# The up stages of a feed-forward block make their own sums of transposed activations

## The chip, the cores and the metric

The program runs on one core of one Trainium2 chip. The metric is the device time of one execution in microseconds (us). TensorE (PE) multiplies, VectorE (DVE) and ScalarE (ACT) prepare its operands and take its results out of PSUM, GpSimd (POOL) does small work and issues some transfers, SyncE (SP) issues most of them. The queues of transfers issued by SP and ACT and the one of POOL are separate, and each engine works through its own instructions in a fixed order.

## What is computed

One layer on 2048 tokens of 1024 values: attention and a recurrent branch (not touched here), then a merge, and a feed-forward block. The part that matters, cut from the reference:

```python
merged = gate_a * (y_a @ proj_a[l]) + gate_b * (y_b @ proj_b[l])
x = x + rms_norm(merged @ w_out[l], post_mix_g[l])

hf = rms_norm(x, pre_ffn_g[l])
u = jnp.square(jax.nn.relu(hf @ w_up[l])) @ w_down[l]
x = x + rms_norm(u, post_ffn_g[l])
```

`hf` is 2048 x 1024, `w_up` 1024 x 4096, all in float32.

## The kernel before

The tokens stand in four groups of 512. For each group the kernel runs its recurrent stage, its attention and its merge (`phase_merge`, which multiplies by `proj_a` and `w_out`). Behind the last group's merge come four stages on halves of two groups: up stage of half 0, down stage of half 0, up stage of half 1, down stage of half 1. The residual steps (`residual_steps`) of a group write the transposed `hf` to DRAM, into `ht[g]`, 128 partitions x 8 blocks x 512 tokens. Those of groups 0 and 1 run beside earlier merges, those of 2 and 3 beside the first down stage.

Float32 operands are split in two parts, `h` and `l` (names that end in `h` and `l`), and each product is three matmuls per block (`mm3`). A split is a cast by ACT and a subtraction by DVE (`split`, or `split_here` where the raw block was loaded into the low part's tile).

An up stage (`phase_up`) multiplies two pairs of column blocks of `w_up` by the two groups of a half with seven products in place of eight. Each takes 12 matmuls, from four blocks of K of 128 rows. On the right-hand side stand two raw halves of the first group (`b1`, tiles `bh` and `bl`), the second group's raw second half (`b22`), and four sums: t1 = g1lo - g0lo, t3 = g1hi - g1lo, t2 = g1hi - t1, t4 = g0hi - t2, where lo and hi are the first and last four blocks of `ht`. The first two products of a step need `bh` and `bl` alone. So the stage begins with eight early pairs of these (the loop over `early`, eight tiles `z`): the first product of a pair is copied to `z` by ACT, the second is added by DVE (`r<-z,ps_u`), and both take turns in two PSUM banks (pool `pd`). Meanwhile the operands of the other five products are made (`operands`), a step or two after each pair. Then comes the main loop with five products per step.

The four sums were made ahead: `combinations` loads four raw blocks of 128 x 512, makes the sums with four subtractions on DVE and stores them in DRAM (`td`) through POOL. That of half 0 runs beside the last group's merge (`early`, with tiles `cmb` in a pool `p1` of its own), that of half 1 beside the first down stage (`beside`). The up stage then loads each sum in two pieces into the low part's tile and splits it there.

`first_half` loads `bl` in four pieces and splits them into `bh` and `bl`. For half 0 it is written behind the merge, ahead of the up stage; for half 1 beside the first down stage. Pools are stacked in on-chip memory, and a tile waits for whatever used its place before. The instructions' order on each engine is set by a scheduler when the program is built, so it is not the order of the code. The last merge's results, four tiles `o0` to `o3` in pool `p0`, are stored to DRAM (`od`) by ACT's queue when the merge is done.

## Time and profile before

| | us |
|---|---|
| median of three runs | 3340.6 (3339.0 to 3341.2) |
| the profiled execution | 3337.6 |
| its span, first to last instruction | 3335.9 |
| last merge, end | about 2034 |
| early pairs of the first up stage | 2034 to 2079 |
| first down stage, end | about 2699 |
| early pairs of the second up stage | about 2699 to 2746 |

The times inside the span are read from the timeline of the profiled execution. Busy time on an engine that is not the bound costs nothing by itself. The waits in front of PE's instructions are what a change can add or take away here. In rows, `L83` is the line in `mm3`, whatever stage calls it, so stages are told apart by tile names: `ps_o` is the merge's product with `w_out`, `ps_u` the up stages', `ps_dn` the down stages'. A row of the waits has the total, the number of times and the longest. In a timeline the bracket at the end of a row gives the engine's idle time before it and what ended it.

### The profile page before, as it was taken

To read this page: it belongs to the slowest core of one execution; us is meant where nothing else is said; L and a number is where in the kernel's file an instruction comes from. 1 tells how busy PE (TensorE), PEld (TensorE's weight loads), DVE (VectorE), ACT (ScalarE), POOL (GpSimd) and SP (SyncE) were. 2 spreads that over 40 slices of the span, in tenths; PEclk is the share of its full clock that TensorE was granted. 3 is DMA by queue.
4 is the path that set the end of the run, shared out by engine and by line. 5 is a ranking of instruction groups with operands and counts; after the bars stand their busy time and mean duration, and the time that the engine had idled before them with its cause. 6 is when DMAs were issued, how large, how long until landed. Compare 5 with 4: busy or idle time off the path is not lost. (4 is left out here: it accounts for less than half of the span.)

```text
span 3335.9 us, 49381 instructions
## 1 busy us (share of the span) xinstructions
PE 3244.5 (97%) x19089; PEld 2608.4 (78%) x19089; DVE 2284.0 (68%) x3814; ACT 1463.2 (44%) x2331; POOL 382.7 (11%) x732
## 2 busy tenths in 40 slices
PE   7999999999999999999999999999999999999998
PEld 6777787777777777777777777888888878888887
DVE  6774656765665774565774675877877787776788
ACT  4434634444644444644434644333431254454432
POOL 2210002111012210012210000111200011100000
PEclk9999999999999999999999999999999999999999
DMA  5224343125263224354224256434756364554444
GB/s 157 80 89 147 98 145 120 61 90 182 91 236 129 69 86 168 106 205 151 83 83 152 87 206 237 131 120 142 268 177 202 106 242 162 169 171 153 141 162 133
DMA packets 166099, 478.43 MB, mean 143 GB/s; under 512 B 17564, under 2 KB 34144, under 8 KB 163176
## 3 DMA queue, kind: packets, MB, share of 16 engines
q1 hardware_dynamic: 110004, 361.97, 32.9%
q0 software_dynamic: 18688, 63.98, 5.0%
q10 hardware_dynamic: 37172, 49.32, 4.1%
q8 instruction: 151, 2.47, 0.3%
q14 instruction: 84, 0.69, 0.1%
HBM read 355.64 MB, written 122.71 MB: 143 GB/s over the span
## 5 line engine op out<-in xcount | busy, mean ns | idle before, releaser
L83 PE MATMUL psd<-hh,whi 128*128 128x512 f32 x1344 | 542.5, 404 | 2.3 <-DVE QA L835 2.3
L83 PE MATMUL psd<-hl,whi 128*128 128x512 f32 x1344 | 539.3, 401 | 0.0
L83 PE MATMUL psd<-hh,wlo 128*128 128x512 f32 x1344 | 536.5, 399 | 0.0
L74 ACT CAST whi<-wraw 128x1024 fp32r<-128x1024 f32 x232 | 243.7, 1050 | 532.7 <-PE psd L83 421.9
L83 PE MATMUL ps_dn<-fop 128*128 128x512 f32 x1920 | 439.7, 390 | 2.1 <-DVE u L1291 1.5
L75 DVE TENSOR_TENSOR wlo<-wraw,whi 128x1024 fp32r<-128x1024 f32 x232 | 283.1, 1220 | 208.9 <-ACT whi L74 188.1
L83 PEld LDWEIGHTS ps_dn<-fop 128*128 128x128 f32 x1920 | 359.4, 188 | 78.6 <-DVE u L1291 2.3
L83 PEld LDWEIGHTS psd<-hh,whi 128*128 128x128 f32 x1344 | 256.1, 191 | 57.5 <-issue 3.4
L83 PEld LDWEIGHTS psd<-hh,wlo 128*128 128x128 f32 x1344 | 255.8, 190 | 54.1 <-issue 3.5
L83 PEld LDWEIGHTS psd<-hl,whi 128*128 128x128 f32 x1344 | 255.8, 190 | 50.8 <-issue 2.1
L83 PE MATMUL ps_dn<-fop,fop 128*128 128x512 f32 x1008 | 228.6, 389 | 0.0
L83 PEld LDWEIGHTS ps_dn<-fop,fop 128*128 128x128 f32 x1008 | 189.3, 188 | 39.2
L1291 DVE TENSOR_TENSOR u<-u,ps_dn 128x512 f32<-128x512 f32 x240 | 160.6, 683 | 54.3 <-PE ps_dn L83 53.8
L895 DVE CUSTOM_DVE_ANT_0 sc<-bias,ps_s 128x640 f32<-128x640 f32 (+4 forms) x128 | 94.1, 735 | 54.6 <-PE ps_s L889 50.6
L74 ACT CAST fop<-wdraw 128x1024 fp32r<-128x1024 f32 x40 | 41.9, 1047 | 191.8 <-DVE u L1291 88.7
L900 ACT ACTIVATE sc<-sc,mn 128x640 f32<-128x640 f32 (+4 forms) x128 | 97.8, 764 | 35.2 <-DVE mn L895 30.1
L74 ACT CAST s12h<-s 128x1024 fp32r<-128x1024 f32 x32 | 33.7, 1054 | 169.5 <-PE ps_u L83 169.5
L1019 PE MATMUL ps_o<-whi,mh 128*128 128x512 f32 x256 | 101.9, 398 | 1.9 <-ACT o L1025 1.9
L83 PE MATMUL ps_p<-yh,whi 128*128 128x512 f32 x256 | 102.1, 399 | 0.7 <-DVE th L985 0.7
L1019 PE MATMUL ps_o<-wlo,mh 128*128 128x512 f32 x256 | 101.8, 397 | 0.7 <-DVE wlo L75 0.7
L83 PE MATMUL ps_p<-yh,wlo 128*128 128x512 f32 x256 | 102.1, 399 | 0.0
L83 PE MATMUL ps_p<-yl,whi 128*128 128x512 f32 x256 | 101.5, 396 | 0.0
(378 smaller groups left out, 6741.8 us busy)
## 6 DMA issues: line engine op xcount, KB each, us to landing
wraw<-in_w_in_dram SPq DMA_DIRECT2D x168, 512.0 KB, 3.7
wraw<-in_w_up_dram SPq DMA_DIRECT2D x80, 512.0 KB, 4.5
ar<-sd SPq DMA_DIRECT2D x21, 1024.0 KB, 4.8
wdraw<-in_w_down_dram SPq DMA_DIRECT2D x40, 512.0 KB, 4.0
araw<-ad SPq DMA_DIRECT2D x40, 512.0 KB, 4.0
gd<-gate ACTq DMA_DIRECT2D x64, 256.0 KB, 2.3
wraw<-in_w_out_dram SPq DMA_DIRECT2D x32, 512.0 KB, 3.7
ad<-r POOLq DMA_DIRECT2D x64, 256.0 KB, 2.4
```

The source lines that it names most:

```text
L74: self.nc.scalar.copy(hi, src)
L75: self.nc.vector.tensor_tensor(lo, src, hi.bitcast(F32), ALU.subtract)
L83: mm = nc.tensor.matmul(ps, l, r, start=start and n == 0, stop=stop and n == last).ins
L895: nc.vector.tensor_tensor_reduce(sc[:, 0:n], bias[:, s0:640], pss[:, c0 : c0 + n], 1.0, 3.0e38, ALU.add, ALU.min, mn,)
L900: nc.scalar.activation(sc[:, 0:n], sc[:, 0:n], AF.Exp, scale=-1.0, bias=mn, accum_out=sm)
L1019: nc.tensor.matmul(ps[t], l[:, k, ts], r[:, k % 2], start=k == 0 and j == 0, stop=k == KB - 1 and j == 2)
L1291: nc.vector.tensor_tensor(u[t][:, ns], u[t][:, ns], ps, ALU.add)
```

## The change

`combinations` and the DRAM tiles `td` are gone, and with them the pool `p1`. Each up stage loads raw blocks: four pieces of 128 x 1024 for the first two blocks of K, issued by SP, and four for the other two, issued by POOL. They go into a second tile of the shape of `z`, `slots`, which existed before in the second up stage only (for sums of its outputs). DVE makes the four sums in place with subtractions of 128 x 1024, with t2 in the last two rows of `z`, and each is split from there. The number of subtracted elements is the same; 4 MB less is stored and 5 MB less loaded in each half.

```diff
--- before.py
+++ after.py
@@ -296,7 +296,6 @@
 
         self.ht = [dp.tile([P, KB, G], F32, name=f"ht{g}") for g in range(self.NG)]
         self.ad = [dp.tile([P, 2, G], F32, name=f"ad{f}") for f in range(FF // P)]
-        self.td = [dp.tile([P, 4, KB // 2, G], F32, name=f"td{h}") for h in range(self.NG // 2)]
         self.sd = [dp.tile([P, len(PARTS), XB, G], F32, name=f"sd{b}") for b in range(BATCHES)]
         self.gd = [dp.tile([P, 2, G], F32, name=f"gd{i}") for i in range(KB)]
         self.yd = [dp.tile([P, G], F32, name=f"yd{p}") for p in range(NP)]
@@ -984,7 +983,7 @@
             self.mm3(ps, [(wh[:, k, c], wl[:, k, c], y[0][:, k], y[1][:, k]) for k in range(NP)])
             nc.vector.scalar_tensor_tensor(t[:, j], t[:, j], 1.0, ps, op0=ALU.add, op1=ALU.mult)
 
-    def phase_merge(self, g, o, between, early=iter(())):
+    def phase_merge(self, g, o, between):
 
         tc, nc, a = self.tc, self.nc, self.a
         with ExitStack() as ctx:
@@ -1001,7 +1000,6 @@
                 self.branches(self.ya, t)
                 nc.vector.tensor_tensor(t, t, self.md[i], ALU.add)
                 self.split(mh[:, 2 * i : 2 * i + 2], ml[:, 2 * i : 2 * i + 2], t)
-                advance(early, 1)
             self.yctx.close()
             self.late = e(tc.tile_pool(name="late", bufs=2, side="right", reuse_waits="tile"))
             for n in range(2):
@@ -1092,22 +1090,6 @@
                     advance(nrm[t], 1)
             yield
 
-    def combinations(self, half, mp, bufs=1):
-
-
-        nc = self.nc
-        KH = KB // 2
-        g0, g1 = (self.ht[2 * half + i] for i in range(2))
-        for k in range(KH):
-            b = mp.tile([P, 4, G], F32, tag="cmb", bufs=bufs, name="cmb")
-            for i, src in enumerate((g0[:, k], g1[:, k], g0[:, KH + k], g1[:, KH + k])):
-                nc.sync.dma_start(b[:, i], src)
-            for o, x, y in ((0, 1, 0), (1, 3, 1), (3, 3, 0), (2, 2, 3)):
-                nc.vector.tensor_tensor(b[:, o], b[:, x], b[:, y], ALU.subtract)
-            nc.gpsimd.dma_start(self.td[half][:, :, k], b)
-            yield
-
-
     def split_here(self, hi, lo):
 
         self.nc.scalar.copy(hi, lo.bitcast(F32))
@@ -1138,20 +1120,23 @@
             bh, bl = self.b1
             B11, B21 = (bh[:, lo4], bl[:, lo4]), (bh[:, hi4], bl[:, hi4])
             z = zp.tile([P, early, G], F32, tag="z", name="z")
+            slots = zp.tile([P, early, G], F32, tag="z", name="slots")
             T = {
                 n: [tb.tile([P, KH, G], F32R, name=n + x) for x in "hl"] for n in ("t4", "b22", "t2", "t3", "t1")
             }
 
             def operands():
-                td, g1 = self.td[half], self.ht[2 * half + 1]
-                for n, src in (
-                    ("t2", td[:, 3]), ("t3", td[:, 1]), ("t1", td[:, 0]), ("b22", g1[:, hi4]), ("t4", td[:, 2])
-                ):
-                    h, l = T[n]
-                    for k in (0, 2):
-                        ks = slice(k, k + 2)
-                        nc.sync.dma_start(l[:, ks].bitcast(F32), src[:, ks])
-                        self.split_here(h[:, ks], l[:, ks])
+                g0, g1 = self.ht[2 * half], self.ht[2 * half + 1]
+                t1, t3, b22, t4 = (slots[:, n : n + 2] for n in range(0, early, 2))
+                t2 = z[:, early - 2 : early]
+                for k in (0, 2):
+                    ks = slice(k, k + 2)
+                    for t, src in ((t1, g0[:, lo4]), (t3, g1[:, lo4]), (b22, g1[:, hi4]), (t4, g0[:, hi4])):
+                        (nc.gpsimd if k else nc.sync).dma_start(t, src[:, ks])
+                    for o, x, y in ((t1, t3, t1), (t2, b22, t1), (t3, b22, t3), (t4, t4, t2)):
+                        nc.vector.tensor_tensor(o, x, y, ALU.subtract)
+                    for n, src in (("t2", t2), ("t3", t3), ("b22", b22), ("t4", t4), ("t1", t1)):
+                        self.split(*(x[:, ks] for x in T[n]), src)
                         yield
 
             def product(l, r, pool, tag):
@@ -1178,7 +1163,6 @@
                 return sums and FIRST <= i < FIRST + BATCHES * XB
 
             if sums:
-                slots = zp.tile([P, early, G], F32, tag="z", name="slots")
                 R = {q: slots[:, n] for n, q in enumerate(("a11", "a12", "a21", "a22", "s1", "s2", "s4"))}
 
             def hidden(src, x, fb, th, out=None):
@@ -1532,13 +1516,10 @@
                 self.phase_rwkv(g)
                 self.phase_attention(g)
                 with ExitStack() as c:
-                    early = iter(())
-                    if g == self.NG - 1:
-                        early = self.combinations(0, c.enter_context(tc.tile_pool(name="p1", bufs=1, reuse_waits="tile")), 2)
                     sp = c.enter_context(tc.tile_pool(name="p0", bufs=2, reuse_waits="tile"))
                     pt = c.enter_context(tc.tile_pool(name="p0p", bufs=2, space=PSUM, reuse_waits="tile"))
                     o = [sp.tile([P, D], F32, tag="o", bufs=GT, name=f"o{t}") for t in range(GT)]
-                    self.phase_merge(g, o, self.after(g, sp, pt), early)
+                    self.phase_merge(g, o, self.after(g, sp, pt))
                     for t in range(GT):
                         self.nc.scalar.dma_start(self.od[g][t], o[t])
             mixing.close()
@@ -1552,7 +1533,6 @@
             def beside(op, pt):
                 for g in (2, 3):
                     yield from self.residuals(g, op, pt)
-                yield from self.combinations(1, op)
                 yield from self.first_half(2, bp)
 
             advance(self.first_half(0, bp))
```

Three places in the order of instructions matter for the prediction. In the rows, a name before the arrow is written and the ones behind it are read; wait names are semaphores: DMAHW of transfers issued by SP and ACT, DMASW of those issued by POOL.

SP at the end of the last merge, before, with the waits (`wraw<-in_w_out` are the merge's weights, `bl<-ht` the first group's raw blocks, `t2l<-td` and `t3l<-td` the stored sums):

```order
L62 DMA wraw<-in_w_out_dram 128x1024 [waits DMAHW2_49,DMAHW0_49,DVE_49]
L1164 DMA wraw<-in_w_up_dram 128x1024 [waits DMAHW3_49,DVE_49]
L1164 DMA wraw<-in_w_up_dram 128x1024 [waits DMAHW4_49,DVE_49]
L62 DMA wraw<-in_w_out_dram 128x1024 [waits DMAHW6_49,DVE_49]
L1121 DMA bl<-ht_335 128x1024 [waits DMASW2_49]
L1121 DMA bl<-ht_335 128x1024 [waits DMAHW5_49]
L1121 DMA bl<-ht_335 128x1024
L62 DMA wraw<-in_w_out_dram 128x1024 [waits DMAHW7_49,DMAHW0_49,DVE_49]
L1121 DMA bl<-ht_335 128x1024
L1164 DMA wraw<-in_w_up_dram 128x1024 [waits DMAHW1_49]
L62 DMA wraw<-in_w_out_dram 128x1024 [waits DMAHW3_49,DMAHW2_49,DVE_49]
L1153 DMA t2l<-td_371 128x1024 [waits DMAHW7_49,PE_49]
```

The same place in the changed program:

```order
L62 DMA wraw<-in_w_out_dram 128x1024 [waits DMAHW5_49,DVE_49]
L62 DMA wraw<-in_w_out_dram 128x1024 [waits DMAHW1_49,DVE_49]
L62 DMA wraw<-in_w_out_dram 128x1024 [waits DMAHW4_49,DVE_49]
L1103 DMA bl<-ht_335 128x1024 [waits DMAHW3_49,DMAHW7_49,DMAHW2_49,Activation_49]
L1103 DMA bl<-ht_335 128x1024
L1103 DMA bl<-ht_335 128x1024 [waits DMAHW5_49]
L1103 DMA bl<-ht_335 128x1024 [waits DMAHW6_49]
L1135 DMA slots<-ht_335 128x1024 [waits DVE_49,PE_49]
L1135 DMA slots<-ht_336 128x1024 [waits DMAHW0_49]
L1135 DMA slots<-ht_336 128x1024 [waits DMAHW1_49]
L1135 DMA slots<-ht_335 128x1024
L1149 DMA wraw<-in_w_up_dram 128x1024 [waits DMAHW3_49,DVE_49]
```

The loads of `bl` stood between the last weights of the merge, and the first waited for a transfer of POOL, the store of `cmb`. Now they stand behind all of them, and the first waits for three transfers of SP or ACT and for ACT. By the semaphores' counts in the built program two of those are the stores `od` of `o0` and `o3`, and the instruction of ACT is the last copy into `o3`. In on-chip memory `bl` lies at 64.7 to 80.7 KB of each partition in both programs; `cmb` lay at 72.7 to 88.7 KB and `o0` to `o3` at 88.7 to 104.7 KB, and now `o0` to `o3` lie at 72.7 to 88.7 KB.

ACT at the end of the last merge, before (`o` are the merge's results, `whi` casts of its weights, `bh` the cast of `bl`, the first four `o` copies are those of the first half of columns):

```order
L74 CAST s12h<-wraw 128x1024
L74 CAST s3h<-wraw 128x1024
L74 CAST whi<-wraw 128x1024 x2
L1113 CAST bh<-bl 128x1024
L1025 COPY o_18791<-ps_o 128x512
L1113 CAST bh<-bl 128x1024
L1025 COPY o_18792<-ps_o 128x512
L1025 COPY o_18793<-ps_o 128x512
L1025 COPY o_18794<-ps_o 128x512
L74 CAST whi<-wraw 128x1024
L1113 CAST bh<-bl 128x1024 x2
L74 CAST whi<-wraw 128x1024 x2
```

and in the changed program, from the last of those four copies to the first up product's copy `z`:

```order
L1023 COPY o_18789<-ps_o 128x512
L74 CAST whi<-wraw 128x1024 x3
L1023 COPY o_18786<-ps_o 128x512
L1524 DMA od_0_331<-o_18786 128x1024
L1023 COPY o_18787<-ps_o 128x512
L1023 COPY o_18788<-ps_o 128x512
L1023 COPY o_18789<-ps_o 128x512
L1524 DMA od_1_332<-o_18787 128x1024
L1524 DMA od_2_333<-o_18788 128x1024
L1524 DMA od_3_334<-o_18789 128x1024
L1095 CAST bh<-bl 128x1024 x4
L1197 COPY z<-ps_u 128x512
```

The casts of `bh` stood ahead of and among the merge's first `o` copies. Now they stand behind all `o` copies and their stores.

DVE in the early part of the first up stage, before (`r<-z,ps_u` ends a pair, `a1l` and `s12l` are weights of coming pairs, `t2l`, `t3l` and `t1l` the low parts of operands):

```order
L1189 TENSOR_TENSOR r<-z,ps_u 128x512
L75 TENSOR_TENSOR a1l<-wraw,a1h 128x1024
L1192 TENSOR_TENSOR r<-r 128x512
L1114 TENSOR_TENSOR t2l<-t2l,t2h 128x1024
L1189 TENSOR_TENSOR r<-z,ps_u 128x512
L75 TENSOR_TENSOR s12l<-wraw,s12h 128x1024
L1192 TENSOR_TENSOR r<-r 128x512
L1114 TENSOR_TENSOR t2l<-t2l,t2h 128x1024
L1114 TENSOR_TENSOR t3l<-t3l,t3h 128x1024
L1189 TENSOR_TENSOR r<-z,ps_u 128x512
L1114 TENSOR_TENSOR t3l<-t3l,t3h 128x1024
L1114 TENSOR_TENSOR t1l<-t1l,t1h 128x1024
```

in the changed program, from the same instruction on:

```order
L1173 TENSOR_TENSOR r<-z,ps_u 128x512
L75 TENSOR_TENSOR a1l<-wraw,a1h 128x1024
L1176 TENSOR_TENSOR r<-r 128x512
L1137 TENSOR_TENSOR slots<-slots 128x1024
L1137 TENSOR_TENSOR z<-slots 128x1024
L1137 TENSOR_TENSOR slots<-slots 128x1024
L1137 TENSOR_TENSOR slots<-slots,z 128x1024
L75 TENSOR_TENSOR t2l<-z,t2h 128x1024
L1173 TENSOR_TENSOR r<-z,ps_u 128x512
L75 TENSOR_TENSOR t3l<-slots,t3h 128x1024
L75 TENSOR_TENSOR b22l<-slots,b22h 128x1024
L1176 TENSOR_TENSOR r<-r 128x512
```

and further on, from the end of the fourth pair to that of the fifth:

```order
L1173 TENSOR_TENSOR r<-z,ps_u 128x512
L75 TENSOR_TENSOR b22l<-slots,b22h 128x1024
L1176 TENSOR_TENSOR r<-r 128x512
L75 TENSOR_TENSOR a1l<-wraw,a1h 128x1024
L1137 TENSOR_TENSOR slots<-slots 128x1024
L1209 TENSOR_TENSOR s_19615<-wraw 128x512
L1137 TENSOR_TENSOR z<-slots 128x1024
L1137 TENSOR_TENSOR slots<-slots 128x1024
L1137 TENSOR_TENSOR slots<-slots,z 128x1024
L75 TENSOR_TENSOR t2l<-z,t2h 128x1024
L1173 TENSOR_TENSOR r<-z,ps_u 128x512
```

Four subtractions and the split of t2 stand between the end of the first pair and that of the second. Four more, with a split and weights, stand between the fourth and the fifth.

## Prediction

> **What bounds the kernel now.** I read the page first, then the busy time by stage, then who TensorE waits for there.
>
> ```profile
> span 3335.9 us, 49381 instructions
> PE 3244.5 (97%) x19089; PEld 2608.4 (78%) x19089; DVE 2284.0 (68%) x3814; ACT 1463.2 (44%) x2331; POOL 382.7 (11%) x732
> ```
>
> TensorE (PE) is busy for 97% of the span and its matmuls are the same before and after, so an edit can only change how long PE waits. The table of stages (length; busy time and count of PE, PEld, DVE, ACT, POOL; granted clock; DMA share; GB/s) shows where such time is to be had in the stages that the change touches: last merge (two rows), early part of the first up stage, the stretch of the first down stage that holds combinations, early part of the second up stage.
>
> ```profile
> 1950.00:1990.00 40.00, 39.68 (x183) 31.61 (x180) 30.85 (x39) 10.88 (x11) 2.17 (x3) 1.00 0.79 282
> 1990.00:2034.20 44.20, 42.03 (x181) 33.48 (x181) 20.76 (x20) 17.31 (x21) 0.71 (x1) 1.00 0.63 235
> 2034.20:2078.90 44.70, 43.74 (x193) 35.87 (x192) 31.33 (x37) 26.60 (x36) 3.80 (x7) 1.00 0.77 284
> 2500.00:2570.00 70.00, 69.59 (x311) 57.28 (x311) 55.80 (x79) 15.08 (x17) 2.92 (x4) 1.00 0.62 211
> 2701.00:2745.80 44.80, 42.21 (x184) 33.98 (x182) 35.62 (x41) 30.39 (x43) 3.54 (x5) 1.00 0.83 309
> ...
> PE ps_o L1019 <- ACT o L1025: 1.9, 2, 1.4
> PE ps_p L83 <- DVE th L985: 0.3, 1, 0.3
> PE ps_o L1019 <- DVE wlo L75: 0.3, 1, 0.3
> ...
> PE ps_dn L83 <- DVE u L1291: 0.4, 1, 0.4
> ```
>
> The stages that lose work have almost no PE idle time to give: 0.3 + 2.2 us in the merge, 0.4 us in the down stage. The waits in the last four rows (three of the merge, one of the down stage: total, times, longest) add up to 2.9 us. The early parts, which receive work, are as full of PE work, and DVE there is busy 31.3 of 44.7 us and 35.6 of 44.8 us.
>
> **What is removed.** 32 subtractions, 32 loads, 8 stores and the 16 loads of stored sums. They lie beside PE work, so their removal is worth at most those 2.9 us. The largest piece, 1.9 us, is ACT's copies of the merge's result, which PE waits for because they are queued behind a cast of `bh`:
>
> ```profile
> 2011.37 1.04 ACT L1113 CAST bh<-bl 128x1024 fp32r<-128x1024 f32 x1 [5.55 <-DMA bl<-ht]
> 2012.32 0.58 ACT L1025 COPY o<-ps_o 128x512 f32<-128x512 f32 x1
> ```
>
> ACT's new order has these copies first, so this goes. The other waits are for DVE work with combinations between its pieces; they go too. Gain: 2.9 us, between 0 and 4 (pipeline refill after each wait included).
>
> **What moves without being named in the change: the loads of `bl`.** `bl` holds the first group's raw blocks for the first up stage. Its place in the partition is 64.7 to 80.7 KB in both programs. Before, the combination buffers `cmb` lay there; now the merge's results `o0` and `o3` (72.7 to 80.7 KB) do, since the pool `p1` below them is gone. The order shows what follows: the first `bl` load waits for two stores on hardware queues (`od` of `o0` and `o3`, by their semaphore values) and for ACT. Before, these loads went out 30 us ahead of need:
>
> ```profile
> 2004.72 1.53 SPq L1121 DMA_DIRECT2D bl<-ht  x3
> 2007.48 0.44 SPq L1121 DMA_DIRECT2D bl<-ht  x1
> ...
> 2033.40 1.64 ACT L1025 COPY o<-ps_o 128x512 f32<-128x512 f32 x3 [0.40 <-PE ps_o L1019]
> 2034.46 2.08 ACTq L1543 DMA_DIRECT2D od<-o  x3
> ...
> L83 PE MATMUL ps_u<-bh,a1h x8: 389/389/389, 2034.3 to 2039.0; 128*128 128x512 f32 x8
> ...
> wraw<-in_w_out_dram SPq DMA_DIRECT2D x32, 512.0 KB, 3.7
> od<-o ACTq DMA_DIRECT2D x16, 512.0 KB, 3.5
> x<-xr POOLq DMA_DIRECT2D x16, 512.0 KB, 4.4
> td<-cmb POOLq DMA_DIRECT2D x8, 1024.0 KB, 5.7
> bl<-ht SPq DMA_DIRECT2D x8, 512.0 KB, 9.8
> ```
>
> PE starts the first up product at 2034.3, straight after the merge's last matmul; the last `o` copy ends at 2035.0, and the last three `od` stores are issued one after the other from 2034.5 on, the last about 2035.5. In the new program, on the same clock: that store lands 3.5 us later (median row), with 0.5 us for the ones ahead of it, 2039.5. The first `bl` load lands 3.7 us after that (the row of a load of this size), 2043.2. ACT casts it (1.04 us), DVE subtracts (1.23 us, the row of 2012.45 below), so the product's second matmul, the first that needs the low part, can go at 2045.4; with the one matmul that went ahead of it (0.2 us) the product starts 10.9 us late. The other three pieces follow about 1.25 us apart (512 KB at the 421 GB/s of the row below), faster than PE uses them. **Wait added: 10.9 us.** Below: the store and the load each at 2.6 us, the fastest landing of an `od` store, give 8. Above: the time from issue to cast of the old `bl` loads, 6.65 us (2004.72 to 2011.37), gives 14. Nothing covers it: PE's next work in order is this product, and every up and down stage stands behind it.
>
> ```profile
> 2012.45 1.23 DVE L1114 TENSOR_TENSOR bl<-bl,bh 128x1024 fp32r<-128x1024 f32 x1 [5.37 <-ACT bh L1113]
> ...
> 2045.40:2050.80 5.40, 5.40 (x25) 4.47 (x24) 1.00 1.03 421
> ...
> L1114 DVE TENSOR_TENSOR bl<-bl,bh x4: 1217/1222/1226, 2012.4 to 2018.6; 128x1024 fp32r<-128x1024 f32 x4
> ...
> L1543 ACTq DMA_DIRECT2D od<-o x4: 326/392/783, 504.7 to 507.0; - x4
> ...
> DMA to landing us min/median/max: 2.6/2.6/2.6
> ```
>
> The Trainium skill ("DMA: Bandwidth & Descriptors", where it derives the bandwidth figures) holds that a core's memory side binds at about 358 GB/s. By it each piece would take 1.46 us, an estimate, and the sum would grow by about 1 us; the row's 421 GB/s speaks against it and decides.
>
> A wait of this length also costs clock. After a wait of 2.84 us elsewhere (its row, then the stretches behind it) the granted clock was half for 6.8 us:
>
> ```profile
> 621.73 1.92 PE L596 MATMUL ps_t<-X,NA 32*32 32x32 f32 x64 [2.84 <-DVE X L575]
> ...
> 621.50:628.30 6.80, 6.58 (x75) 0.50 0.15 58
> 628.30:635.10 6.80, 6.80 (x118) 1.00 0.28 80
> ```
>
> Half of 6.8 us is 3.4; some of it falls while PE waits for the second piece anyway, so I take **2 us**, between 0 and 3.4. The Trainium skill ("TensorE: Matmul & The Clock Gate", on the HAM clock gate) gives one busy window of about 3.4 us at half clock, which by itself would be 1.7 us (an estimate); the row is longer.
>
> **What is added on DVE.** In each up stage eight subtractions of 128x1024 enter the early part, where PE runs eight pairs of products of 5.49 us. One costs 1.22 us, 1.14 when another follows (the starts in DVE's timeline below); 9.1 us in all, against DVE idle time of 13.4 and 9.2 us in the stage rows, of which one pair's length is its wait for the first pair. The average nearly fits; the order doesn't. DVE's `r<-z,ps_u` frees the second of two banks, and PE needs it 2.74 us into the next pair but one product later.
>
> ```profile
> 2050.85 0.69 DVE L1189 TENSOR_TENSOR r<-z,ps_u 128x512 f32<-128x512 f32 x1 [0.21 <-PE ps_u L83]
> 2051.45 1.22 DVE L1114 TENSOR_TENSOR t3l<-t3l,t3h 128x1024 fp32r<-128x1024 f32 x1
> 2052.59 1.22 DVE L1114 TENSOR_TENSOR t1l<-t1l,t1h 128x1024 fp32r<-128x1024 f32 x1
> ...
> 2072.54 0.69 DVE L1189 TENSOR_TENSOR r<-z,ps_u 128x512 f32<-128x512 f32 x1 [0.89 <-PE ps_u L83]
> ...
> 2078.03 0.69 DVE L1189 TENSOR_TENSOR r<-z,ps_u 128x512 f32<-128x512 f32 x1 [3.42 <-PE ps_u L83]
> ...
> 2716.50 0.69 DVE L1189 TENSOR_TENSOR r<-z,ps_u 128x512 f32<-128x512 f32 x1 [2.11 <-PE ps_u L83]
> ...
> 2721.93 0.69 DVE L1189 TENSOR_TENSOR r<-z,ps_u 128x512 f32<-128x512 f32 x1 [3.42 <-PE ps_u L83]
> ```
>
> First up stage, counted from the end of pair 0: `r`, `a1l`, the square, four subtractions, `t2l` and the next `r` take 0.6+1.14+0.6+4.56+1.14+0.69 = 8.7 us; PE wants the bank at 5.49+2.74 = 8.2: 0.5 us of wait. The second four stand between `r` of pair 3 (done at 18.1) and `r` of pair 4: six operations of 128x1024 and two blocks of 0.6 ahead of `t2l` and `r`, 9.9 us, so 28.0 against 0.5+22.0+2.74 = 25.2: 2.8 us. Together **3.3 us**. Second up stage, from `r` of pair 2 at 2716.5: 0.6, eight operations of 1.14 and `r` end at 2726.9; pair 3 ends at 2721.9 and the bank is wanted at 2724.6. ACT's copy of `z` behind the new casts holds the first product too; pair 4 ends 2.7 us late, of which 1.3 us replaces an old wait. The second four then hold `r` of pair 5 to 2740.7 against 2737.9. Together **4.2 us**. The lower bound of both is 0, if the loads are early and the order slacker than counted. The upper: the second set of raw blocks is loaded through POOL, the last only after `t1l` has been read out. I counted 4.4 us to landing, the row of POOL's 512 KB transfers; at 9.8 us, the worst load row, 4 us more each, 7.3 and 8.2.
>
> **Sum.** -2.9 + 10.9 + 2 + 3.3 + 4.2 = +17.5 us. The profiled execution took 3337.6 us in all (span 3335.9), so 3355.1 there; the median of the three runs is 3.0 us above that execution, so I say 3358. With all ends low (gain 4): 8 - 4 = +4; with all high: 14+3.4+7.3+8.2 = +33.
>
> **Rivals.** Forecast: wait, clock and both backlogs, 3358, chance 0.5. *Wait without backlog*: DVE's idle time (13.4 and 9.2 us) covers the 9.1 us; for it stand the averages, against it the counted order: 3340.6 - 2.9 + 10.9 + 2 = 3351, chance 0.24. *POOL's loads late*: the second four subtractions stand in DVE's queue for `t1`, and everything behind them: 3358 + 8 = 3366, chance 0.17. *Relief only* (not slower): the loads of `bl` still come early. It decides at one point, which transfers the two semaphore values of the held load stand for: if they were older ones than `od` of `o0` and `o3`, the loads would go out behind the last `w_out` load (2017.5 in the row below) and land 10 us ahead of need. Then 3340.6 - 2.9 = 3337.7, with DVE covered; counting the semaphores' updates in the built program speaks against it, chance 0.05. *Small wait*: 8 us, no clock loss, no backlog, 3346; chance 0.04.
>
> ```profile
> 2017.54 0.33 SPq L62 DMA_DIRECT2D wraw<-in_w_out_dram  x1
> ```
>
> **Range and chances.** A difference of 0.2%, 6.7 us, is about what a measurement of this kernel tells from no change, so slower begins at 3347.3. Forecast and late loads lie wholly above, the wait alone for nine parts in ten: 0.87 slower, 0.11 within, 0.02 faster. The ends of the sum are 3345 and 3374; the range, 3346 to 3369, leaves out relief, the far end of late loads and what needs several low or high ends at once.
>
> **What would show it.** The first `bl` load issued after 2036 on the old clock instead of 2004.7, and a PE wait of 8 to 14 us ahead of the first `ps_u<-bh` product, with a granted clock of 0.5 behind it; no 1.9 us wait of `ps_o` for ACT; in each early part one or two PE waits of 1 to 3 us ended by `r<-z,ps_u`; merge and down stages otherwise unchanged. If the first up product follows the merge at once, the main term is wrong; if PE's early parts show no wait for `r`, the backlog is.

## The result and the profile after

The changed kernel takes 3368.0 us (median of four runs, 3366.3 to 3369.6) against 3340.4 us before: 27.6 us more, ratio 1.0084 with a 95% interval of 1.0068 to 1.0100. It is slower, inside the range, and 10 us slower than forecast.

The page of the changed kernel: PE has the same 19089 matmuls and is busy for 8.1 us longer than before (3244.5 us there). The rest of the added time went into waits.

```profile
span 3367.9 us, 49344 instructions
PE 3252.6 (97%) x19089; PEld 2613.7 (78%) x19089; DVE 2284.4 (68%) x3798; ACT 1465.5 (44%) x2331; POOL 380.4 (11%) x732
```

To see where, both traces are cut at the same matmuls (length; busy time and count of PE, PEld, DVE, ACT, POOL; granted clock; DMA share; GB/s). The rows are the last merge (first to last product `ps_o`), the first early part (to the first product with `t2h`), the first down stage with what follows it up to the second up stage, and the second early part (first product of that stage to the first with `t2h`). Before:

```profile
1987.33:2034.03 46.70, 44.53 (x192) 35.54 (x191) 23.43 (x23) 18.20 (x22) 0.71 (x1) 1.00 0.64 238
2034.03:2078.90 44.87, 43.91 (x194) 36.04 (x192) 31.33 (x37) 26.77 (x36) 3.80 (x7) 1.00 0.77 285
...
2340.18:2693.44 353.26, 351.07 (x1577) 290.19 (x1576) 281.94 (x367) 98.52 (x132) 34.05 (x66) 1.00 0.56 186
2693.44:2745.85 52.41, 49.77 (x218) 40.15 (x216) 43.04 (x53) 35.07 (x57) 7.24 (x12) 1.00 0.84 309
```

And in the changed kernel:

```profile
1988.37:2031.69 43.32, 43.32 (x192) 35.85 (x191) 15.19 (x13) 14.94 (x18) 0.00 (x0) 1.00 0.44 152
2031.69:2097.77 66.08, 48.36 (x195) 38.09 (x193) 45.14 (x49) 31.24 (x40) 6.01 (x11) 0.90 0.58 204
...
2359.02:2710.16 351.14, 350.45 (x1578) 290.37 (x1577) 273.91 (x351) 98.41 (x132) 30.27 (x62) 1.00 0.50 164
2710.16:2773.84 63.68, 53.21 (x218) 41.71 (x216) 52.54 (x61) 36.21 (x57) 9.45 (x16) 0.95 0.69 236
```

The profiled spans differ by 32.0 us (3367.9 - 3335.9). Merge -3.4, first early part +21.2, down stage -2.1, second early part +11.3 give 27.0. Another 3.9 us lie behind the last matmul (the section on the closing drain has its cause). The remaining 1.1 us are spread over stretches without a changed instruction, 1.0 of it ahead of this merge. (The two profiled executions stand 1.7 above their median and 2.8 us below theirs, hence 32.0 here and 27.6 between the medians.)

The rows also divide what each early part grew by. In the first, PE's busy time is 4.4 us longer and its idle time 16.8 us; in the second, 3.4 and 7.8 us. The matmuls are the same and the granted clock is below 1 in both (0.90 and 0.95), so the longer busy time is an estimate of what the lower clock cost there (the ends of matmuls are modelled).

What ended PE's waits in the changed kernel (total, times, longest):

```profile
PE ps_u L83 <- ACT z L1197: 13.9, 5, 4.9
PE ps_u L83 <- ACT bh L1095: 10.4, 1, 10.4
...
PE ps_u L83 <- DVE r L1173: 1.6, 2, 1.0
...
PE ps_u L83 <- DVE bl L1096: 0.5, 1, 0.5
```

The wait for `bh` is one wait in one place; the waits for the copies `z` are five, in both early parts. The merge's waits for ACT's `o` are gone. The timeline around the wait for `bh`:

```profile
2037.47 1.75 SPq L1103 DMA_DIRECT2D bl<-ht  x4
2039.32 2.12 SPq L1135 DMA_DIRECT2D slots<-ht  x4
2041.43 1.04 ACT L1095 CAST bh<-bl 128x1024 fp32r<-128x1024 f32 x1 [8.73 <-DMA bl<-ht]
...
2042.52 0.80 PE L83 MATMUL ps_u<-bh,a1h 128*128 128x512 f32 x1 [10.45 <-ACT bh L1095]
...
2043.79 0.80 PE L83 MATMUL ps_u<-bl,a1h 128*128 128x512 f32 x1 [0.47 <-DVE bl L1096]
```

All four `bl` loads leave together at 2037.5, behind the stores of the merge; the first cast comes 4.0 us later, and PE at once behind it.

The second thing to see is a wait for `z` in the first early part. DVE and ACT there:

```profile
2075.69 1.23 DVE L1137 TENSOR_TENSOR slots<-slots 128x1024 f32<-128x1024 f32 x1 [1.88 <-DMA slots<-ht]
...
2076.95 1.04 ACT L74 CAST t1h<-slots 128x1024 fp32r<-128x1024 f32 x1 [4.53 <-DVE slots L1137]
2077.90 1.04 ACT L74 CAST s12h<-wraw 128x1024 fp32r<-128x1024 f32 x1
2078.85 1.04 ACT L74 CAST t2h<-z 128x1024 fp32r<-128x1024 f32 x1
2079.90 1.04 ACT L74 CAST t3h<-slots 128x1024 fp32r<-128x1024 f32 x1
2080.85 0.58 ACT L1197 COPY z<-ps_u 128x512 f32<-128x512 f32 x1
...
2081.48 0.80 PE L83 MATMUL ps_u<-bh,s3h 128*128 128x512 f32 x1 [4.89 <-ACT z L1197]
```

DVE's subtraction waits for a raw block, ACT's cast `t1h` for DVE, three more casts stand behind that one, and only then comes the copy that frees PE's bank.

### The profile page after: what moved, and what is told of

It is laid out like the page before. It is cut to its first block, busy times and chain, and to the rows that moved or that the text cites. A ratio compares the mean times of both kernels' runs of the same rounds, so it can differ in the third digit from the quotient of the medians.

```text
span 3367.9 us, 49344 instructions
## 1 busy us (share of the span) xinstructions
PE 3252.6 (97%) x19089; PEld 2613.7 (78%) x19089; DVE 2284.4 (68%) x3798; ACT 1465.5 (44%) x2331; POOL 380.4 (11%) x732
```

## The experiments

Every kernel below was profiled and its trace cut as above. The table has each stage's length minus that of before, in us; "rest" is the second up stage's main loop up to the second down stage, "end" what follows the last matmul. Ahead of the last merge the traces differ by several us (1983 to 1994 us), which the cuts leave out, so the table tells more than the ratios do. It has one execution of each kernel, though: the merge of e3_second, whose code is that of before, came out 2.1 us longer, so a difference of 1 or 2 us counts only where it repeats.

| kernel | merge | first early | down | second early | rest | end | ratio to before (95%) |
|---|---|---|---|---|---|---|---|
| changed kernel | -3.4 | 21.2 | -2.1 | 11.3 | -0.2 | 3.9 | 1.0084 (1.0068 to 1.0100) |
| e1_place | -3.4 | 6.6 | -2.1 | 10.9 | -0.9 | 4.0 | 1.0032 (1.0019 to 1.0045) |
| e2_layout | -2.4 | 14.0 | 1.2 | 0.3 | -1.0 | 0.2 | 1.0034 (1.0021 to 1.0047) |
| e3_second | 2.1 | 0.0 | -1.6 | 9.7 | -0.1 | 4.9 | 1.0028 (1.0016 to 1.0041) |
| e4_direct | -3.4 | 17.1 | -2.1 | 7.2 | -0.3 | 2.9 | 1.0066 (1.0049 to 1.0083) |
| e5_direct_place | -3.4 | 9.9 | -1.3 | 7.5 | -0.2 | 2.9 | 1.0034 (1.0022 to 1.0046) |
| e6_spread | -3.4 | 6.8 | -2.1 | 11.2 | 0.8 | 3.2 | 1.0030 (1.0020 to 1.0041) |
| e7_fill | -3.4 | 23.1 | -2.1 | 9.7 | -0.3 | 4.2 | 1.0080 (1.0065 to 1.0095) |
| e8_td_sp | -3.3 | 0.0 | -0.1 | 1.0 | 1.5 | 3.3 | one run |
| e9_banks | -3.4 | 8.3 | -1.9 | -1.9 | 5.6 | 4.2 | 1.0014 (1.0004 to 1.0023) |
| e10_pool_sub | -3.4 | 8.2 | -1.4 | 12.7 | 1.2 | 3.9 | 1.0039 (1.0024 to 1.0054) |
| e11_all | -3.4 | 10.1 | -1.1 | 11.7 | -0.3 | 3.0 | 1.0035 (1.0021 to 1.0049) |
| e12_before_sp | -3.4 | 0.0 | -0.7 | -2.3 | 1.4 | 3.2 | 0.9985 (0.9977 to 0.9994) |

### The place of the merge's results

The side effect undone in the changed kernel:

```diff
+if g == self.NG - 1:
+    hold = c.enter_context(tc.tile_pool(name="p1", bufs=1, reuse_waits="tile"))
+    hold.tile([P, 8, G], F32, tag="cmb", name="hold")
 sp = c.enter_context(tc.tile_pool(name="p0", bufs=2, reuse_waits="tile"))
```

> The changed kernel with an unused 16 KB tile in the pool p1 of the last group, so that the merge's results o lie at 88.7 KB again and not in the place of bl; nothing else differs. Theory (the 10.4 us wait ahead of the first up product comes from o0 and o3 lying in bl's place, and costs clock behind it): the first bl load goes out before the merge ends, the wait is gone, and the time falls by 10.8 + about 2.5 us from 3368 to about 3355; the waits for z in the two early parts stay. Rival 1 (the wait only moves work: DVE and ACT used it to catch up, and their backlog now costs what it saved): 3362 to 3368, with longer waits for z or r in the first early part. Rival 2 (the loads come late because of their order on SP's queue, not their place): 3368, no change.

The side effect alone, in the kernel before:

```diff
-early = self.combinations(0, c.enter_context(tc.tile_pool(name="p1", ...)), 2)
 sp = c.enter_context(tc.tile_pool(name="p0", bufs=2, reuse_waits="tile"))
...
+early = self.combinations(0, c.enter_context(tc.tile_pool(name="p1", ...)), 2)
 self.phase_merge(g, o, self.after(g, sp, pt), early)
```

> The kernel before, with stored combinations and all, but with the pool p1 opened after the pool p0, so that o0 and o3 lie at 72.7 to 80.7 KB, in bl's place, and cmb above them; this is the side effect of the change alone. Theory (place alone makes the wait): a wait of about 10 us ahead of the first up product and half clock behind it, 3340.4 + 10.8 + 2.5 = about 3353.5. Rival (the wait needs the moved work too, or the combinations' loads hide it): 3340 to 3345.

With the place held, the wait for `bh` is gone and the first early part falls from +21.2 to +6.6 (by the same division, 3.9 us of idle time and 2.7 of busy time). The place alone gives +14.0 there, with every subtraction still where it was. PE's wait there, and the row of that early part:

```profile
PE ps_u L83 <- ACT bh L1113: 10.6, 1, 10.6
...
2032.83:2091.67 58.84, 46.77 (x195) 37.54 (x193) 35.78 (x41) 30.92 (x40) 3.79 (x7) 0.88 0.70 253
```

Against the row of before (44.87 and 43.91), 11.1 of the 14.0 us are idle time, which is this wait and 0.5 us for `bl`, and 2.9 us are longer busy time.

Both directions agree on 14.0 to 14.6 us, so the place makes the wait. Neither rival holds: the other stages are as in the changed kernel (second early part +10.9 with the place held), and combinations do not hide the wait. The last merge is 2.4 us shorter in e2 as well, with all combinations still in it: the casts of `bh` no longer stand ahead of ACT's `o` copies. So the relief of the merge comes mainly from ACT's order, not from the removed subtractions.

### One half alone

Only the second up stage makes its own sums:

```diff
-ops = operands()
+ops = operands_raw() if sums else stored()
...
-yield from self.combinations(1, op)
```

> The kernel before with the change made for the second half alone: the second up stage makes its own sums from raw blocks, the combinations of the first half stay in the last merge. The place of bl is that of before. Account of the changed kernel's trace: the waits for z in the second early part (9.0 us in four waits) and half clock behind them add about 11 us, the down stage gives 0.4 back: 3351. The recorded sum: 4.2 us of backlog, 3344.6. Rival (the stage differs because of what the late first up stage left behind): under 3344.

The second early part is 9.7 us longer by itself, so its delay owes little to the first half (9.7 to 11.3 us where both halves are changed); the recorded 4.2 us is less than half of it.

### The loads of the raw blocks

```diff
-t1, t3, b22, t4 = (slots[:, n : n + 2] for n in range(0, early, 2))
-t2 = z[:, early - 2 : early]
+raw = {n: T[n][1].bitcast(F32) for n in T}
+t1, t2, t3, t4 = (slots[:, n : n + 2] for n in range(0, early, 2))
...
-(nc.gpsimd if k else nc.sync).dma_start(t, src[:, ks])
+nc.sync.dma_start(raw[n][:, ks], src[:, ks])
```

> The changed kernel with the raw blocks loaded straight into the low halves of the operands t1, t3, b22 and t4 by SP, which wait for no earlier reader, instead of into the slots, the second set by POOL. The subtractions and casts keep their order and number. Theory 1 (the loads of the second set land 7 to 8.5 us after issue, and that holds DVE's subtractions, ACT's casts and the z copies behind them): the waits for z shrink to what DVE's own work makes, by the recorded terms 3.3 and 4.2 instead of about 8 and 11, so 3368 - 11.5 = about 3356. Rival 1 (ACT's and DVE's order decides, five casts and four subtractions stand ahead of the z copy whenever they run): 3364 to 3368. Rival 2 (without late loads DVE's idle time covers all of it): 3368 - 19 = 3349.

In the changed kernel the transfers of POOL's set took 7.0 us from issue to landing, by the view of DMA issues:

```profile
slots<-ht POOLq DMA_DIRECT2D x8, 512.0 KB, 7.0
```

With direct loads the early parts are 4.2 and 4.1 us shorter than in the changed kernel. Beyond the 14.0 of the place that leaves 3.1 and 7.2 us. In the first part the largest of the waits left is 2.1 us for the split `s12l`; in the second they are for `r` (3.8) and `z` (2.2). In the whole kernel:

```profile
PE ps_u L83 <- DVE r L1186: 4.4, 2, 3.8
PE ps_u L83 <- ACT z L1210: 2.2, 2, 1.5
```

So late loads look like a part of the backlog, as theory 1 has it, but not all of it. The profiled execution is the fastest of the four, 6.8 us below their median (3366.4 us), and the intervals of 1.0066 and 1.0084 overlap, so the ratio does not show the gain.

Both edits together:

> The changed kernel with both earlier edits: raw blocks loaded straight into the operands' low halves by SP, and the unused tile in p1 that keeps o out of the place of bl. Theory (what is left of the backlog is DVE's own work, 3.1 us in the first and 7.2 us in the second early part, as in the trace of the direct loads; merge and down stage give 5.9 us, the end costs about 3 to 4): 3343 (before, on the last chip) - 5.9 + 3.1 + 7.2 + 3.5 = about 3351, or 1.002 to 1.003 of before. Rival (the direct loads only helped because the 10.8 us wait ahead gave them time): as with the place alone, 1.0032 or more, with waits for z of 3 to 5 us back in the first early part.

The second early part repeats (+7.5). The first gets worse, +9.9 instead of 6.6, by a new wait in one place:

```profile
PE ps_u L83 <- DVE s12l L75: 5.5, 1, 5.5
```

DVE's timeline shows why. Behind its last idle time, 0.56 us, it works without a gap, and the split of the weights that PE needs stands behind three subtractions of the second set, whose loads are no longer late:

```profile
2050.13 0.69 DVE L1186 TENSOR_TENSOR r<-z,ps_u 128x512 f32<-128x512 f32 x1 [0.56 <-PE ps_u L83]
...
2052.47 1.22 DVE L1144 TENSOR_TENSOR slots<-t3l,t1l 128x1024 f32<-128x1024 f32 x1
2053.60 1.22 DVE L1144 TENSOR_TENSOR slots<-b22l,t3l 128x1024 f32<-128x1024 f32 x1
2054.74 1.22 DVE L1144 TENSOR_TENSOR slots<-b22l,slots 128x1024 f32<-128x1024 f32 x1
2055.88 1.22 DVE L75 TENSOR_TENSOR s12l<-wraw,s12h 128x1024 fp32r<-128x1024 f32 x1
```

Neither expectation named this: earlier loads let the sums go ahead of what PE needs sooner. It also means that the 3.1 us of e4 hold only behind the long wait for `bh`: with the place held, the same loads make the first early part longer, not shorter.

### The order of the subtractions, the banks and the engine

Spread subtractions, on top of the last kernel:

```diff
-for o, x, y in ((t1, r3, r1), (t2, b22, t1), (t3, b22, r3), (t4, r4, t2)):
-    nc.vector.tensor_tensor(o, x, y, ALU.subtract)
-for n, src in (("t2", t2), ("t3", t3), ("b22", None), ("t4", t4), ("t1", t1)):
+for n, src, subs in (("t1", t1, ((t1, r3, r1), (t2, b22, t1))), ("t2", t2, ((t4, r4, t2),)), ("t3", t3, ((t3, b22, r3),)), ("b22", None, ()), ("t4", t4, ())):
+    for o, x, y in subs:
+        nc.vector.tensor_tensor(o, x, y, ALU.subtract)
```

> As the kernel with direct loads and the place, but with the subtractions spread between the casts: t1 and t2's ahead of the first cast, then one ahead of each of the next two, none ahead of the last two. Number of operations and bytes are the same. Theory (the order inside the burst decides: four subtractions and up to two casts ahead of r, where PE waits): the waits for r and z shrink from 3.1 and 7.2 to 0 to 2 and 1 to 4 us, 1.000 to 1.0015 of before. Rival (DVE has too little idle time in the second early part, in any order): the second early part stays 6 to 8 us longer than before, 1.002 to 1.003.

The order is not the answer: the first early part gains 3.1 us on e5, the second loses 3.7. The rival holds in kind: in the second early part DVE works without idle time for 25 us behind its last wait for a raw block (from 2724.9). But 11.2 us is more than the 6 to 8 it named.

Four banks for the second product of each early pair, with the place held and the loads of the changed kernel:

```diff
-hidden(z[:, i], product(A12, B21, self.pd, "d"), 2 * i, 0)
+hidden(z[:, i], product(A12, B21, pn, "dn"), 2 * i, 0)
```

> The changed kernel with the unused tile in p1 (o out of the place of bl), and the second product of each early pair in the pool of four banks that the later products use, instead of the two banks of pd; same loads, subtractions and casts. Theory (PE's waits in the early parts are waits for a bank that r or the copy z still holds, so that room to run ahead covers the late loads): the waits for z and r all but go, the first early part is 0 to 3 us longer than before instead of 6.6, the second 2 to 6 instead of 10.9: 3344 - 5.9 + 1.5 + 4 + 4 = about 3348, 1.001 of before. Rival (the weights' casts and subtractions of the next pair are queued behind the same work, so the waits only change their name to the operands a, s12 and s3): both parts as with the place alone, 1.003.

In the second stage PE now runs through the early part (-1.9 us), and the main loop behind it is 5.6 us longer, by waits for its operands and by busy time (2.8 us each). Early part and rest together are +3.7 instead of +9.9 in e1, so most of what that stage lost was waiting for a bank that `z` or `r` still held. In the first stage the rival is right: the waits have only changed their name.

```profile
PE ps_u L83 <- DVE s12l L75: 6.1, 2, 4.1
```

The same with the second stage's subtractions on POOL:

```diff
-nc.vector.tensor_tensor(o, x, y, ALU.subtract)
+(nc.gpsimd if sums else nc.vector).tensor_tensor(o, x, y, ALU.subtract)
```

> As the kernel with more banks, with the eight subtractions of the second up stage on POOL instead of DVE; those of the first stay on DVE. POOL has rows of 1.39 us for 128x512 subtractions elsewhere, so about 2.8 us each here. Theory (in the second early part DVE's own work is the limit: 35.6 of 44.8 us before, 9.1 added): the second early part is 0 to 3 us longer than before, below that of the kernel with more banks, though each chain of four subtractions takes 11 us; 1.000 of before. Rival (the loads and the chain's latency decide, not DVE's share): the chain of four on POOL takes 11 instead of 4.6 us, the products of t wait for it, and the second early part is 6 to 15 us longer than before.

The early pairs run almost without a wait, as with the four banks alone, and PE then waits once, ahead of the main loop. POOL's row and PE's:

```profile
L1137 POOL TENSOR_TENSOR slots<-slots 128x1024 f32<-128x1024 f32 x4 | 10.5, 2632 | 17.3 <-DMA out_dram<-u 9.8 <-DMA slots<-ht 7.5
...
PE ps_u L83 <- ACT s12h L74: 15.0, 1, 15.0
```

The chain of sums must end within the early part wherever it runs; at 2.6 us a subtraction it does not. Nor was DVE freed: it is busy for 53.1 us in this part, against 43.0 before, with as many instructions. The six splits that ran beside POOL's subtractions took 2.33 to 3.36 us each, the others 1.21 or 1.22:

```profile
2728.77 3.38 POOL L1137 TENSOR_TENSOR slots<-slots,z 128x1024 f32<-128x1024 f32 x1
...
2729.92 3.31 DVE L75 TENSOR_TENSOR t3l<-slots,t3h 128x1024 fp32r<-128x1024 f32 x1
2733.15 1.21 DVE L75 TENSOR_TENSOR b22l<-slots,b22h 128x1024 fp32r<-128x1024 f32 x1
```

So this run does not test the theory: what POOL took over (9.1 us) came back on DVE as slower splits (9.8 us).

Direct loads, four banks and the place together, and `o` moved over t2, which no load writes (`hold` 40 KB):

> The changed kernel with direct loads, with four banks for the second early product, and with 40 KB of unused tile in p1, so that o lies at 112.7 to 128.7 KB, over t2 alone, which no load writes; so neither bl nor a raw block waits for a store of o. Theory (late loads hold DVE's queue in the first early part, banks cover the rest): no wait for bh, waits for s12l under 2 us, the first early part 0 to 3 us longer than before, second early part and the down stage behind it together 0 to 4 us longer, merge and down stage 5.9 us shorter, the end 3.2 us longer: 0.9995 to 1.001 of before. Rival (DVE's nine added microseconds cost their length in the first early part wherever they stand): first early part 6 to 9 us longer, 1.0015 to 1.003.

Still both early parts are 10.1 and 11.7 us longer. In the first, PE's largest waits are 3.2 us for ACT's `a1h` and 2.1 us for `s12l`. In the second, its wait for `s12l` is one wait:

```profile
PE ps_u L83 <- DVE s12l L75: 11.7, 1, 11.7
```

There DVE works without idle time from its first `s` of that stretch to `s12l`, 26 us later, with all eight subtractions of the sums between them. The first of these rows is late by a load of weights, which stands on SP's queue with the raw blocks (though the kernel of e12, below, has 4.9 us of the same wait and no longer early part):

```profile
2726.74 0.69 DVE L1222 TENSOR_TENSOR s<-wraw 128x512 f32<-128x512 f32 x1 [4.63 <-DMA wraw<-in_w_up_dram]
...
2753.12 1.21 DVE L75 TENSOR_TENSOR s12l<-wraw,s12h 128x1024 fp32r<-128x1024 f32 x1
```

The rival holds here in kind, though 10.1 us is more than its 6 to 9: in the second part DVE's queue is full, and PE waits for whatever stands last in it.

### The clock behind the wait

```diff
+if g == self.NG - 1:
+    spare = po.tile([P, 512], F32, tag="o", name="spare")
+    for j in range(40):
+        nc.tensor.matmul(spare, mh[:, KB - 1, :P], wh[:, 1], start=j == 0, stop=j == 39)
```

> The changed kernel with 40 matmuls of mh and whi into an unused bank of the merge behind its last product; nothing reads them, and they run while PE waits for bh. Theory (the wait costs its own length and then about 2 us of half clock, since PE had been idle): PE's clock stays 1.0 through the wait, the product starts when it did, and the first early part is 1.5 to 2.5 us shorter than the changed kernel's, 66.1 us from the merge's last product to the first product of t2. Rival (the low clock comes from something else in this place, such as the DMA traffic of 4 MB): half clock stays and the time is that of the changed kernel or 0 to 1 us more.

The filler keeps the clock at 1.0 until it ends, but a gap of 1.4 us for `bh` is left before the product and one of 0.8 us for `bl` behind its first matmul, and the clock falls to half there (windows of 2 us, columns as above):

```profile
2034.00:2036.00 2.00, 2.00 (x10) 1.65 (x10) 0.00 (x0) 0.00 (x0) 0.00 (x0) 1.00 1.00 399
...
2044.00:2046.00 2.00, 1.64 (x4) 1.35 (x5) 1.67 (x3) 1.38 (x2) 0.00 (x0) 0.54 1.00 401
2046.00:2048.00 2.00, 2.00 (x7) 1.54 (x6) 1.97 (x2) 1.04 (x1) 0.00 (x0) 0.60 0.99 401
```

The first early part is not shorter (67.9 us against 66.1). Traffic did not lower the clock here, since the filler ran at 1.00 at a DMA share of 1.00 (first row). This run can't say what the low clock costs behind the wait, since it came back: the theory is neither shown nor refuted. The row of e2 above gives that price, 2.9 us of busy time.

### The closing drain, and a version that beats both

In the stretch behind the last matmul one instruction differs by microseconds, POOL's closing drain. Its row before (nanoseconds: shortest, median, longest):

```profile
L1603 POOLq DRAIN  x3: 40/93/1582, 3330.1 to 3335.3; - x3
```

In the changed kernel:

```profile
L1583 POOLq DRAIN  x3: 40/143/8524, 3358.3 to 3367.7; - x3
```

The kernel before with its stores of combinations on SP:

```diff
-nc.gpsimd.dma_start(self.td[half][:, :, k], b)
+nc.sync.dma_start(self.td[half][:, :, k], b)
```

> The kernel before, with the eight stores of combinations issued by SP instead of POOL; nothing else differs. In the trace of the changed kernel the last matmul is followed by 13.98 us to the end of the span, before by 10.05; the difference is POOL's closing drain, 8.52 us instead of 1.58. Theory (the drain hangs on how many or which DMAs POOL has issued): the drain takes about 8 us here too, since the kernel with direct loads, with the same 184 POOL DMAs, shows 7.87, and the span grows by 3 to 4 us. Rival (the drain hangs on the second up stage's new order): 1.6 us as before.

```profile
L1603 POOLq DRAIN  x3: 40/102/7872, 3336.1 to 3344.5; - x3
```

The theory holds: the drain takes 7.87 us with nothing changed but which DMAs POOL issues. It does not follow their number, since before and after both have 192. What of them it follows stays open. This kernel also shows the whole relief of the merge, -3.3 us, without any subtraction moved out of it.

With only the first half's stores on SP, and four banks:

```diff
-nc.gpsimd.dma_start(self.td[half][:, :, k], b)
+(nc.gpsimd if half else nc.sync).dma_start(self.td[half][:, :, k], b)
...
-hidden(z[:, i], product(A12, B21, self.pd, "d"), 2 * i, 0)
+hidden(z[:, i], product(A12, B21, pn, "dn"), 2 * i, 0)
```

> The kernel before, with stored combinations, but with those of the first half stored by SP instead of POOL (the second half's stay on POOL), and with four banks for the second early product. It asks how much of what the change wanted is to be had without moving the subtractions. Theory: the last merge 3.3 us shorter, as with all eight stores on SP, the early parts 0 to 2 us shorter, the end 3 to 4 us longer if POOL's closing drain grows with 188 DMAs as it did with 184, or unchanged if it stays at 1.6 us: 0.998 to 1.000 of before. Rival (the relief of the merge comes back as waits in the first early part, since PE gets there sooner and its operands do not): 1.000 to 1.001.

3337.2 us against 3343.3, ratio 0.9985 (0.9977 to 0.9994), in spite of a drain of 8.2 us: by a little, 0.15%, faster than the kernel before, and so than the changed one. The merge keeps its -3.4 us and the first early part is to the hundredth what it was, so the rival falls. Two of ACT's four copies of `o` in the merge's middle now stand ahead of the first cast of `bh`, and that cast does not wait (before, all four stood behind one that had waited 5.55 us for its load):

```profile
2007.01 1.07 ACT L1025 COPY o<-ps_o 128x512 f32<-128x512 f32 x2
2007.96 1.06 ACT L1113 CAST bh<-bl 128x1024 fp32r<-128x1024 f32 x1
2008.91 1.09 ACT L1025 COPY o<-ps_o 128x512 f32<-128x512 f32 x2
```

## Why the prediction was right, and where it was off

**Relief, -2.9.** Right in direction, too small: -3.4 in the merge and -2.1 in the down stage, 5.5 together, above the upper end of 4. In the merge the reason given for the largest piece, ACT's order, is what e2 and e8 show.

**Wait for `bl`, +10.9, and half clock, +2.** Right: waits of 10.4 and 0.5 us, ended by ACT's `bh` and DVE's `bl`, where they were expected. The place alone, e2, costs 14.0 against 12.9 for the two terms: 11.1 of idle time against 10.9, and 2.9 of longer busy time against 2. This is the term on which the forecast rests, and its mechanism is shown in both directions (e1 and e2).

**Backlog in the first early part, +3.3.** Too small: 21.2 - 14.0 = 7.2 us (5.6 of idle and 1.6 of busy time), 6.6 in e1 (3.9 and 2.7). One step that failed is "I counted 4.4 us to landing, the row of POOL's 512 KB transfers": they took 7.0 (median). The block that the late subtraction waited for was issued at 2067.1, and the subtraction began at 2075.7. The rule in the Trainium skill ("DMA: Bandwidth & Descriptors", on the anatomy of a SWDGE transfer: 2.0 us plus the bytes at 436 GB/s) would make it 3.2 us, an estimate; the row is more than twice that. With early loads (e4) 3.1 us are left, but that this is close to 3.3 is luck: it needs the long wait ahead, and without it (e5) the same loads gave 9.9. The clock is the other step: the text has a loss of clock behind the wait for `bl`, none behind the waits of the backlog. The signs also named the wrong wait. They put down one or two waits of 1 to 3 us to `r<-z,ps_u`, with "no wait for `r`" as the mark of a wrong backlog; PE waited for `r` 1.0 us here and 0.5 us in the second part, and mainly for the copy `z`, which stands behind casts that wait for the same subtractions.

**Backlog in the second early part, +4.2.** The term furthest off: 11.3 us, 9.7 to 11.3 in all kernels with the same loads and banks, and 7.2 to 7.5 even with early loads in the same order. It exceeds the upper end (8.2) too. (That end adds "4 us more each" for a landing of 9.8 in place of 4.4; the difference of the two rows is 5.4, but with it the end is 9.6, still below.) The text names ACT's copy `z` for one pair; in the trace it ended four waits, 9.0 of 10.4 us, and e9 shows that with two more banks most of the loss goes. Of the 11.3 us, 7.8 are idle time and 3.4 busy time: these backlog waits of 4 us lower the clock as the long wait does. Behind the one ended by `z` at 2761.3:

```profile
2763.00:2765.00 2.00, 2.00 (x6) 1.61 (x5) 2.00 (x2) 1.26 (x2) 0.00 (x0) 0.50 0.00 0
2765.00:2767.00 2.00, 2.00 (x6) 1.52 (x6) 0.25 (x1) 0.00 (x0) 0.00 (x0) 0.50 0.62 190
```

**The average of DVE's idle time.** The rival "wait without backlog" rested on 13.4 us idle in the first early part. Of its 13.5 us (44.87 - 31.33), 5.9 lie ahead of DVE's first `r` at 2039.97, since the part begins at 2034.03; 7.6 are left for 9.1 us of subtractions. It was refuted in every version: with its subtractions on DVE, no remedy brought the first early part below 6.6 us once the place was held.

**The end, 0.** Not foreseen: 3.9 us by POOL's drain.

**The sum.** Against the sum of 17.5 us the two traces differ by 32.0. The 14.5 us between are 11.0 of backlog (3.9 and 7.1), 3.9 of the end, 1.1 of the place and 1.1 elsewhere, less 2.6 of relief. The measured 3368.0 lies 1.0 us inside the upper end of the range, 3369, and that it lies inside is luck: what was mis-sized or not foreseen adds 17.1 us one way and takes 2.6 the other.

The rival "POOL's loads late" (3366) was the nearest in time and right on the loads, but priced them alone; "relief only" and "wait without backlog" fell. That both early parts suffer from one shortage, of DVE time ahead of PE's needs, is supported where DVE worked without a gap ahead of PE's wait (e5, e6, e11), but not shown: no run freed DVE, since e10 slowed its splits instead. How much of the 7.2 and 11.3 us of backlog is DVE's, ACT's or the loads' stays open.

## What to carry to other kernels

A buffer that is removed moves the ones above it in the stack: look up which tile lies in whose place, since a load can then wait for a store that it has nothing to do with. Idle time of an engine counts only where it lies behind the moved work's inputs and ahead of its reader, and each piece of work is placed in the queue of every engine that touches it, not only of the one that does the sum. When a stage gets shorter by removing work, first ask whether the same relief is to be had by another queue: here moving stores from POOL to SP gave all of the merge's. And an engine is not freed by moving work to another until its own instructions beside that work are seen to take no longer.

## What the runs showed of the hardware

POOL's closing drain took 1.58 us in the kernel before and in e2, which has the same POOL DMAs, and 7.87 to 9.4 us in every kernel whose POOL DMAs differed from it; the time was the same to 0.01 us in kernels with the same POOL DMAs (7.87 in five kernels with 184, 8.52 or 8.53 in five with the changed kernel's 192).

At one stall the loss of clock came in two sizes. The stall at 1740 us (PE waits 3.8 us for DVE), which no change touches, in the kernel before:

```profile
1740.00:1760.00 20.00, 16.08 (x207) 12.58 (x207) 11.48 (x32) 10.66 (x19) 1.17 (x2) 0.91 0.31 112
```

and in the changed kernel:

```profile
1740.00:1760.00 20.00, 16.21 (x182) 12.76 (x181) 12.17 (x34) 9.74 (x17) 1.17 (x2) 0.83 0.40 131
```

20 us at 0.91 or 0.83 have lost 1.8 or 3.4 us of clock, so 3.6 or 6.8 us were at half clock, in part while PE stood idle. In the other twelve traces the same 20 us have 0.91 or 0.83 as well, but for one, whose stall comes later and is cut by the window (0.87). The long wait of e2 lost more, 7.1 us (58.84 us at 0.88). The Trainium skill ("TensorE: Matmul & The Clock Gate", Part 1, on what is actually happening) has a free-running window of 3.4 us, and the two amounts agree with one and two of them. It also has at least one idle window, about 3.4 us, ahead of the fall; in e7 PE was idle for 1.4 us and then, between two matmuls, for 0.8, so there the measurement differs.
